# Where the two operands of a matmul lie in SBUF: a two-layer decoder trunk whose feed-forward stages get new start addresses

## The chip, the cores and the metric

The kernel runs on one core of a Trainium2 chip, in one launch. The metric is the device time of that core in microseconds (us), as the median of several runs. The engines that matter here are TensorE (PE in the profile; its weight loads have a row of their own, PEld), VectorE (DVE), ScalarE (ACT) and the DMA queue that SyncE (SP) issues.

## The reference, cut to what matters

The program is a decoder trunk of two layers on 256 tokens with a model width of 1024. Each layer is a half-step feed-forward block, a mixer and a second half-step feed-forward block. So there are four feed-forward blocks, and they hold most of the arithmetic:

```
def swiglu(x, w_gate, w_up, w_down):
    return (jax.nn.silu(x @ w_gate) * (x @ w_up)) @ w_down
...
        h = h + 0.5 * swiglu(rms_norm(h, ffn1_norm_g[layer]), ffn1_w_gate[layer],
                             ffn1_w_up[layer], ffn1_w_down[layer])
        hn = rms_norm(h, mix_norm_g[layer])
...
        h = h + jnp.concatenate([primary, mem_out], axis=-1) @ w_o[layer]
        h = h + 0.5 * swiglu(rms_norm(h, ffn2_norm_g[layer]), ffn2_w_gate[layer],
                             ffn2_w_up[layer], ffn2_w_down[layer])
```

The inner width of a block is 2816, so `w_gate` and `w_up` are 1024 x 2816 and `w_down` is 2816 x 1024, all float32. The mixers are a convolution beside attention to a memory (layer 0) and block attention beside attention to a memory (layer 1). A key and value projection stands between the layers.

## The kernel before, in words

**Split operands.** Every large product is made in float32r from a high and a low part of each operand. A weight arrives by DMA in chunks of 128 x 2048 (tile `raw`), and each half of a chunk becomes a tile `wh` (high part, written by ACT in line 214) and a tile `wl` (what is left, written by DVE in line 218), both 128 x 1024, four buffers each. The activations are held transposed, tokens along the free axis, as tiles with a high and a low part side by side: `y` with eight k-slices of 2 x 256 elements (function `y_tiles`), and `hs`, the gated inner activations, with 22 such slices.

**The matmuls of a feed-forward block.** `mm2` makes one k-step of one output tile from two matmuls. The first has a 128 x 128 block of `wh` as its stationary operand and streams the whole slice of `y` or `hs`, high and low part: 512 columns. The second has the block of `wl` and streams the high part alone: 256 columns. These are called the hi step and the lo step here. Each matmul needs its own stationary block, so hi steps and lo steps alternate and a weight load stands between any two matmuls. A block has 22 gate tiles and 22 up tiles of 8 k-steps (352 pairs), and 8 output tiles of the down product with 22 k-steps. Seven of these use `mm2` (154 pairs), and the last uses `mm3`: three matmuls of 256 columns per k-step, with stationary `wh`, `wh`, `wl` (66 matmuls). The names in the profile are `ag`, `au`, `ao` for gate, up and down of the first block, and `b`, `c`, `d` for the others. All matmuls go through a helper in line 183.

**Other matmuls.** In the mixers and the key and value projections (`A`, `B`, `C`, `Q`, `M`, `mkv`, `kv`, `mqJ`, `b0J` to `b2J`) the roles are the other way round: a block of the activations is the stationary operand, and `wh` or `wl` is streamed, 512 or 256 columns at a time. The two output projections (`oao`, `obo`) use `mm3` with weights stationary and the tile `cat` streamed, 256 columns each.

**Where the tiles lie.** `y_tiles` allocates a buffer that is 128 elements longer than needed and starts the data `at` elements in: 8 by default, 0 for `ay0`, `by0` and the memory tiles, 16 for `cy0`. The build lays the tiles out so. Addresses are in bytes within a partition, modulo 512, and in brackets modulo 128:

| operand | base | start before |
|---|---|---|
| `wh`, all four buffers | 288 | 288 (32) |
| `wl`, all four buffers | 288 | 288 (32) |
| `y0`, `oay`, `by1`, `oby`, `cat` | 288 | 320 (64) |
| `hs` of the four blocks | 192 | 192 (64) |
| `ay0`, `by0`, `my` | 288 | 288 (32) |
| `cy0` | 288 | 352 (96) |

k-slices are 2048 bytes apart and weight blocks 512 bytes, so every step of a stage has the same places modulo 512.

**Order.** The four blocks are traced in a scheduler's order. The two mixers are written out by hand (`MIX0`, `MIX1`), and there the steps named `hi16` to `hi19` of `MIX1` already convert the first weights of the fourth block.

Of the kernel before, what the change touches and what calls it, by code (L numbers as in the profile page):

```python
# [10 lines left out]
F32R = mybir.dt.float32r  # L11
# [6 lines left out]
P = 128  # L18
DM = 1024
KD = DM // P  # L20
SEQ = 256
NT = SEQ // P
DFF = 2816
KF = DFF // P
# [14 lines left out]
HC = 1024  # L39
# [70 lines left out]
NSPEC = 4 * PW  # L110

Y_AT = {"ay0": 0, "by0": 0, "cy0": 16}

@with_exitstack
def tile_kernel(ctx: ExitStack, tc: tile.TileContext, w, xT, memT, pos, vec, hg, const, wave, bias, taps, out):
    nc = tc.nc
    cp = ctx.enter_context(tc.tile_pool(name="cp", bufs=1))
    wp = ctx.enter_context(tc.tile_pool(name="wp", bufs=3))
# [32 lines left out]
    nc.vector.memset(mhalf, -0.5)  # L151


    state = {"chunk": 0, "half": 0, "raw": None, "order": "", "last": {}, "between": None, "made": []}

    def behind(i, other):
        tc.add_manual_dep(i.ins, other.ins.name,
# [11 lines left out]
    def A(i):  # L169
        return in_order("A", i)  # L170

    def V(i):
        return in_order("V", i)
# [4 lines left out]
    def tables(func):  # L178

        behind(A(nc.scalar.activation(warm, onec, func)), state["func"])  # L180

    def mmul(*a, **k):
        return in_order("P", nc.tensor.matmul(*a, **k))  # L183
# [7 lines left out]
    def load_chunk(n):  # L191
        if n == 0:
            return raw0
        raw = wp.tile([P, CH], F32, name=f"raw{n}", tag="raw", bufs=3)
        if n < 3:
            nc.sync.dma_start(raw[:, :HC], w[n][:, :HC])
            state["sync"] = nc.sync.dma_start(raw[:, HC:], w[n][:, HC:])
        else:
            state["sync"] = nc.sync.dma_start(raw, w[n])
        return raw  # L200

    def half_hi():
        n, h = state["chunk"], state["half"]
        if h == 0:
            state["raw"] = load_chunk(n)
        raw = state["raw"][:, h * HC:(h + 1) * HC]
        wh = wp.tile([P, HC], F32R, name=f"wh{n}_{h}", tag="wh", bufs=4)
        wl = wp.tile([P, HC], F32R, name=f"wl{n}_{h}", tag="wl", bufs=4)
        state["chunk"], state["half"] = (n, 1) if h == 0 else (n + 1, 0)
        q = HC // 2 if n < 2 else HC  # L210
        parts = [slice(c, c + q) for c in range(0, HC, q)]

        def hi(s):
            state["act"] = nc.scalar.activation(wh[:, s], raw[:, s], AF.Copy)  # L214
            return state["act"]

        def lo(s):
            state["dve"] = nc.vector.tensor_tensor(wl[:, s], raw[:, s], wh[:, s].bitcast(F32), op=ALU.subtract)  # L218
            return state["dve"]
        return wh, wl, parts, hi, lo  # L220
# [16 lines left out]
    def mm3(o, wt, y, k, first, last, **kw):  # L237
        h, l = wt
        i = mmul(o, h, y[:, k, 0], start=first, stop=False, **kw)
        mmul(o, h, y[:, k, 1], start=False, stop=False, **kw)  # L240
        mmul(o, l, y[:, k, 0], start=False, stop=last, **kw)
        return i

    def mm2(o, wt, y, k, first, last, turn=None):

        h, l = wt
        a = mmul(o, h, y[:, k].rearrange("p a s -> p (a s)"), start=first, stop=False)
        if turn is not None:
            state["between"] = a
            turn()  # L250
            last_turn, state["between"] = state["between"], None
        b = mmul(o[:, :SEQ], l, y[:, k, 0], start=False, stop=last)
        if turn is not None:
            behind(b, last_turn)
# [9 lines left out]
    def both_halves(name, o, tag):  # L264

        c = tp.tile([P, SEQ], F32, name=name + "c", tag="cvq")
        nc.scalar.activation(c, o[:, SEQ:], AF.Copy)
        a = tp.tile([P, SEQ], F32, name=name, tag=tag)
        nc.vector.tensor_tensor(a, o[:, :SEQ], c, op=ALU.add)
        return a  # L270

    def mm3_tok(o, wh, wl, y, t, k, c, first, last):
        s = slice(t * P, (t + 1) * P)
        mmul(o, y[:, k, 0, s], wh[:, c], start=first, stop=False)
        mmul(o, y[:, k, 0, s], wl[:, c], start=False, stop=False)
        mmul(o, y[:, k, 1, s], wh[:, c], start=False, stop=last)

    def psum(name, tag="mm", bufs=4):
        return ps.tile([P, 512], F32, name=name, tag=tag, bufs=bufs)


    def y_tiles(name, at=8):

        n = KD * 2 * SEQ
        y = yp.tile([P, n + P], F32R, name=name, tag="y")
        return y[:, at:at + n].rearrange("p (k h s) -> p k h s", k=KD, h=2)
# [11 lines left out]
    def square_sum(name, acc, src, first, adder=nc.gpsimd):  # L298
        if first:
            nc.scalar.activation(acc, src, AF.Square)  # L300
        else:
            sq = tp.tile([P, SEQ], F32, name=name, tag="sq")
            nc.scalar.activation(sq, src, AF.Square)
            adder.tensor_tensor(acc, acc, sq, op=ALU.add)
# [32 lines left out]
    def new_acc(name):  # L337
        return tp.tile([P, SEQ], F32, name=name, tag="acc")

    def ffn(name, y, acc, nexts, store=False, hook=None, after=None, hook_down=None, r=None, plan=None):  # L340


        plan = plan or {}
        rows_at = [j for (j, _, _), what in plan.items() if what == "rows"]
        hs = cp.tile([P, KF, 2, SEQ], F32R, name=name + "hs", tag="hs")
        first = acc is None
        rb = None if r is None else bcast_rows(name + "nb", r)
        halves = {}
# [22 lines left out]
        for j in range(KF):  # L371
# [4 lines left out]
            if first and j == 0:  # L376
# [21 lines left out]
                n = KD  # L398
# [9 lines left out]
            else:  # L408

                at = ("sc", 2) if first and j == 2 else ()  # L410
# [21 lines left out]
            for i in sorted(halves):  # L432
                g, h = halves.pop(i)
                if i > 1 or not rows_at:
                    g, h = both_halves(f"{name}gs{i}", g, "g"), (lambda i=i, h=h: both_halves(f"{name}h{i}", h, "h"))
                gated(i, g, h, rb)
        if after:
            tables(after)
        ys = [y_tiles(f"{name}y{i}", Y_AT.get(f"{name}y{i}", 8)) for i in range(len(nexts))]
        acc = new_acc(name + "acc")  # L440
        it = tiles_of(KD * KF // 8)
        for m in range(KD):
            po = psum(f"{name}o{m}")
            if hook_down:
                with tc.issue_after(state["act"].ins):
                    hook_down(m)

            both_sums = m < KD - 1
            for k in range(KF):
                if both_sums:  # L450
                    mm2(po, next(it), hs, k, k == 0, k == KF - 1)
                else:
                    mm3(po[:, :SEQ], next(it), hs, k, k == 0, k == KF - 1)
            if both_sums:
                d = both_halves(f"{name}d{m}", po, "g")
                nc.vector.scalar_tensor_tensor(d, d, 0.5, rb, op0=ALU.mult, op1=ALU.mult)
            else:
                d = tp.tile([P, SEQ], F32, name=f"{name}d{m}", tag="g")
                nc.vector.scalar_tensor_tensor(d, po[:, :SEQ], 0.5, rb, op0=ALU.mult, op1=ALU.mult)
            nc.vector.tensor_tensor(x[:, m], d, x[:, m], op=ALU.add)  # L460
            if store:
                nc.sync.dma_start(out[m], x[:, m])
                continue
            for yy, g in zip(ys, nexts):
                state["ends"] = scaled_split(yy, x[:, m], m, g)
            square_sum(f"{name}q{m}", acc, x[:, m], m == 0)
        return ys, acc

    def heads_norm(name, t, n):
# [32 lines left out]
    def proj(name, y, *uses):  # L502

        os_ = [psum(f"{name}{t}") for t in range(NT)]
        n = MW * len(uses)
        per = HC // n
        for k0 in range(0, KD, per):
            wh, wl = half_chunk()
            for t in range(NT):
                for i in range(per):  # L510
                    k = k0 + i
                    mm3_tok(os_[t][:, :n], wh, wl, y, t, k, slice(i * n, (i + 1) * n), k == 0, k == KD - 1)
        for t in range(NT):
            for i, use in enumerate(uses):
                use(t, os_[t][:, i * MW:(i + 1) * MW])
# [193 lines left out]
    y = y_tiles("y0")  # L709
# [123 lines left out]
    for i in range(HEAD1):  # L833
        @step(f"hi{i}")
        def _(i=i):
            halves[i] = half_hi()
            for s in halves[i][2]:
                j = A(halves[i][3](s))
            if i == HEAD0 + 1:
                behind(j, state["ends"][0])  # L840
# [291 lines left out]
    ys = y_tiles("oay")  # L1132
# [6 lines left out]
    y = ys  # L1139
# [17 lines left out]
    ys = y_tiles("oby")  # L1157
# [4 lines left out]
    for i in range(20):  # L1162
        @step(f"hi{i}")
        def _(i=i):
            halves[i] = half_hi()
            for s in halves[i][2]:
                j = A(halves[i][3](s))
            if i == 4:
                behind(j, state["ends"][0])
            if i >= 16:  # L1170
                state["made"].append(halves[i][:2])

        @step(f"lo{i}")
        def _(i=i):
            for s in halves[i][2]:
                j = V(halves[i][4](s))

            if i == 3:
                behind(j, state["ends"][1])
# [167 lines left out]
    y, acc = ys, sums  # L1347
# [162 lines left out]
```

## Time and profile before

| | us |
|---|---|
| median of 3 runs | 959.43 |
| lowest and highest | 958.76, 960.69 |
| the profiled execution, its own time | 958.8 |
| its span, first to last instruction | 956.8 |
| PE busy | 950.2 |
| PEld busy | 833.0 |
| DVE busy | 719.1 |
| ACT busy | 561.8 |

The profile is of one execution. The spans of matmuls overlap, because a matmul starts before the one before it has drained. So the length of one row is not what a matmul costs: that is the distance from its start to the start of the next, called a step here. The chain of work that ended last merges matmuls that follow each other into pieces, and a piece divided by its count is the mean step.

### The profile page before, as it was taken

The page shows a single profiled execution, that of the slowest core. Times are in us where ns is not written, and L with a number is a line of the kernel's source. Part 1 is how long each engine was busy: PE and PEld are TensorE (multiplying, and loading weights), DVE is VectorE, ACT ScalarE, POOL GpSimd, SP SyncE. Part 2 cuts the span into 40 slices and gives each one's busy share as a digit, 9 for nine tenths or more (in the row PEclk, how much of TensorE's full clock was granted, in tenths as well). Part 3 has the DMA queues.
Part 4 walks back from the last instruction along what each step waited for, and adds up shares of the span by engine and source line. Part 5 has one row for each costly group of instructions (what it writes and reads, how often), then busy time and mean ns, then how long its engine had stood idle before and what let it go on. Part 6 is the DMA issues. An engine that isn't in the chain of part 4 may idle for free.

```text
span 956.8 us, 15067 instructions
## 1 busy us (share of the span) xinstructions
PE 950.2 (99%) x5699; PEld 833.0 (87%) x5699; DVE 719.1 (75%) x1243; ACT 561.8 (59%) x1026; POOL 103.1 (11%) x101
## 2 busy tenths in 40 slices
PE   9999999999999999999999999999999999999998
PEld 6888888888789888888988888888997998888887
DVE  7888877767887877767767777767779578777663
ACT  6676666554566665555556665555548666556442
POOL 0122000112223000001123000000134120000000
PEclk9999999999999999999999999999999999999999
DMA  8755555554334655555555455555542245555560
GB/s 326 272 197 181 176 190 205 178 182 170 133 132 166 216 191 179 195 199 176 192 194 188 176 187 205 181 183 202 187 177 79 99 176 188 208 177 184 199 215 19
DMA packets 26936, 174.16 MB, mean 182 GB/s; under 512 B 3376, under 2 KB 5136, under 8 KB 6512
## 3 DMA queue, kind: packets, MB, share of 16 engines
q1 hardware_dynamic: 26576, 173.04, 51.4%
q8 instruction: 44, 0.72, 0.3%
q14 instruction: 28, 0.23, 0.1%
q10 hardware_dynamic: 288, 0.17, 0.1%
HBM read 172.15 MB, written 1.05 MB: 181 GB/s over the span
## 4 chain that ended last, share of the span: by engine, by line
PE 96%; DVE 3%; ACT 0%; POOL 0%; issue 0%; ACTq 0%
PE ag L183 6%; PE au L183 6%; PE do L183 6%; PE co L183 6%; PE bo L183 6%; PE ao L183 6%; PE bg L183 6%; PE dg L183 6%; PE cg L183 6%; PE cu L183 6%; PE bu L183 6%; PE du L183 6%; PE kv L183 3%; PE obo L183 2%; PE oao L183 2%; PE A L183 1%
## 5 line engine op out<-in xcount | busy, mean ns | idle before, releaser
L214 ACT ACTIVATE wh<-raw 128x1024 fp32r<-128x1024 f32 (+1 forms) x326 | 341.8, 1050 | 339.5 <-PE dg L183 26.8
L218 DVE TENSOR_TENSOR wl<-raw,wh 128x1024 fp32r<-128x1024 f32 (+1 forms) x326 | 396.5, 1218 | 178.2 <-ACT wh L214 176.9
L183 PE MATMUL ag<-y,wh 128*128 128x512 f32 x176 | 63.7, 396 | 0.0
L183 PE MATMUL au<-y,wh 128*128 128x512 f32 x176 | 63.2, 392 | 0.0
L183 PE MATMUL bg<-oay,wh 128*128 128x512 f32 x176 | 62.4, 391 | 0.0
L183 PE MATMUL dg<-oby,wh 128*128 128x512 f32 x176 | 62.4, 391 | 0.0
L183 PE MATMUL bu<-oay,wh 128*128 128x512 f32 x176 | 62.2, 390 | 0.0
L183 PE MATMUL du<-oby,wh 128*128 128x512 f32 x176 | 62.2, 390 | 0.0
L183 PE MATMUL cg<-by,wh 128*128 128x512 f32 x176 | 62.2, 391 | 0.0
L183 PE MATMUL cu<-by,wh 128*128 128x512 f32 x176 | 62.1, 391 | 0.0
L183 PE MATMUL bo<-bhs,wh 128*128 128x512 f32 (+1 forms) x198 | 61.1, 367 | 0.0
L183 PE MATMUL ao<-ahs,wh 128*128 128x512 f32 (+1 forms) x198 | 61.1, 367 | 0.0
L183 PE MATMUL co<-chs,wh 128*128 128x512 f32 (+1 forms) x198 | 61.1, 367 | 0.0
L183 PE MATMUL do<-dhs,wh 128*128 128x512 f32 (+1 forms) x198 | 61.1, 367 | 0.0
L183 PE MATMUL cg<-by,wl 128*128 128x256 f32 x176 | 49.8, 283 | 0.0
L183 PE MATMUL bg<-oay,wl 128*128 128x256 f32 x176 | 49.7, 282 | 0.0
L183 PE MATMUL dg<-oby,wl 128*128 128x256 f32 x176 | 49.7, 282 | 0.0
L183 PE MATMUL du<-oby,wl 128*128 128x256 f32 x176 | 49.6, 282 | 0.0
L183 PE MATMUL cu<-by,wl 128*128 128x256 f32 x176 | 49.6, 282 | 0.0
L183 PE MATMUL bu<-oay,wl 128*128 128x256 f32 x176 | 49.6, 282 | 0.0
L183 PE MATMUL ag<-y,wl 128*128 128x256 f32 x176 | 49.6, 284 | 0.0
L183 PE MATMUL au<-y,wl 128*128 128x256 f32 x176 | 49.4, 283 | 0.0
(948 smaller groups left out, 2309.6 us busy)
## 6 DMA issues: line engine op xcount, KB each, us to landing
raw<-in_w SPq DMA_DIRECT2D x158, 1024.0 KB, 4.8
raw<-in_w SPq DMA_DIRECT2D x5, 512.0 KB, 8.2
mT<-in_memT SPq DMA_DIRECT2D x1, 1024.0 KB, 8.3
out<-x SPq DMA_DIRECT2D x8, 128.0 KB, 1.8
raw<-in_w SPq DMA_DIRECT2D x2, 256.0 KB, 4.0
x<-in_xT SPq DMA_DIRECT2D x1, 512.0 KB, 6.6
spec<-in_bias SPq DMA_DIRECT2D x1, 384.0 KB, 9.8
tapw<-in_taps SPq DMA_DIRECT2D x1, 288.0 KB, 9.1
```

Source lines behind the costliest of these rows:

```text
L183: return in_order("P", nc.tensor.matmul(*a, **k))
L214: state["act"] = nc.scalar.activation(wh[:, s], raw[:, s], AF.Copy)
L218: state["dve"] = nc.vector.tensor_tensor(wl[:, s], raw[:, s], wh[:, s].bitcast(F32), op=ALU.subtract)
```

## The change

Three places get new start addresses. `y_tiles` starts its data 16 elements in by default (64 bytes, before: 32). The gated activations `hs` start 40 elements in (160 bytes, before: 0), in a tile that is 512 bytes longer. The tiles `wl` are 512 bytes longer, and in the feed-forward blocks their data starts 16 elements in. A variable in `state` switches that on at the start of a block and off at its end; the projections that `proj` makes in the middle of a block switch it off for themselves, and the last four conversions of `MIX1`, which belong to the fourth block, switch it on.

```
-    def y_tiles(name, at=8):
+    def y_tiles(name, at=16):
...
 Y_AT = {"ay0": 0, "by0": 0, "cy0": 16}
+LOW_AT, GATED_AT = 16, 40
...
         wh = wp.tile([P, HC], F32R, name=f"wh{n}_{h}", tag="wh", bufs=4)
-        wl = wp.tile([P, HC], F32R, name=f"wl{n}_{h}", tag="wl", bufs=4)
+        wl = wp.tile([P, HC + P], F32R, name=f"wl{n}_{h}", tag="wl", bufs=4)[:, state["low_at"]:state["low_at"] + HC]
...
+        state["low_at"] = LOW_AT
         plan = plan or {}
         rows_at = [j for (j, _, _), what in plan.items() if what == "rows"]
-        hs = cp.tile([P, KF, 2, SEQ], F32R, name=name + "hs", tag="hs")
+        n = KF * 2 * SEQ
+        hs = cp.tile([P, n + P], F32R, name=name + "hs", tag="hs")
+        hs = hs[:, GATED_AT:GATED_AT + n].rearrange("p (k h s) -> p k h s", k=KF, h=2)
...
-        ys = [y_tiles(f"{name}y{i}", Y_AT.get(f"{name}y{i}", 8)) for i in range(len(nexts))]
+        ys = [y_tiles(f"{name}y{i}", Y_AT.get(f"{name}y{i}", 16)) for i in range(len(nexts))]
...
+        state["low_at"] = 0
         return ys, acc
...
+        low_at, state["low_at"] = state["low_at"], 0
         for k0 in range(0, KD, per):
             wh, wl = half_chunk()
...
+        state["low_at"] = low_at
...
+            if i >= 16:
+                state["low_at"] = LOW_AT
             halves[i] = half_hi()
```

The build then has these starts modulo 512 (modulo 128 in brackets); `wh`, `ay0`, `by0`, `my` and `cy0` keep theirs:

| operand | base after | start after |
|---|---|---|
| `wl` in the feed-forward blocks | 288 | 352 (96) |
| `wl` elsewhere | 288 | 288 (32) |
| `y0`, `oay`, `by1`, `oby`, `cat` | 288 | 352 (96) |
| `hs` of the four blocks | 192 | 352 (96) |

On every engine the same instructions stand in the same order as before.

More of the change, by code (lines that the diff above doesn't have):

```diff
@@ L151, in tile_kernel @@
     nc.vector.memset(mhalf, -0.5)
-    state = {"chunk": 0, "half": 0, "raw": None, "order": "", "last": {}, "between": None, "made": []}
+    state = {"chunk": 0, "half": 0, "raw": None, "order": "", "last": {}, "between": None, "made": [], "low_at": 0}
     def behind(i, other):
```

## The prediction

> **What bounds the kernel now.** I read the page first: the busy shares, the granted clock and the chain of work that ended last.
>
> ```profile
> span 956.8 us, 15067 instructions
> PE 950.2 (99%) x5699; PEld 833.0 (87%) x5699; DVE 719.1 (75%) x1243; ACT 561.8 (59%) x1026; POOL 103.1 (11%) x101
> ...
> PEclk9999999999999999999999999999999999999999
> ...
> PE 96%; DVE 3%; ACT 0%; POOL 0%; issue 0%; ACTq 0%
> ```
>
> TensorE is 96% of the chain, at full clock from end to end. There is hardly a wait to remove, so the time moves only if matmuls follow each other faster or slower. Since "a busy PE is not PE at its peak", the next view is the chain in order of time, where a piece divided by its count is the mean step from one matmul's start to the next. First a stretch of the second block's gate and up products, where a piece of 16 is eight pairs of a hi and a lo step:
>
> ```profile
> 321.11 2.77 PE bu L183 x16
> 323.88 2.77 PE bg L183 x16
> 326.65 2.77 PE bu L183 x16
> ```
>
> 2.77 / 8 = 346.3 ns per pair, piece after piece without a gap. Then the timeline of PE and its weight loads in the fourth block, to see what runs beside a stream:
>
> ```profile
> 886.12 0.39 PE L183 MATMUL dg<-oby,wh 128*128 128x512 f32 x1
> 886.12 0.19 PEld L183 LDWEIGHTS dg<-oby,wl 128*128 128x128 f32 x1
> 886.35 0.28 PE L183 MATMUL dg<-oby,wl 128*128 128x256 f32 x1
> 886.35 0.19 PEld L183 LDWEIGHTS dg<-oby,wh 128*128 128x128 f32 x1
> 886.47 0.39 PE L183 MATMUL dg<-oby,wh 128*128 128x512 f32 x1
> ```
>
> When the hi step starts streaming 512 columns of `oby`, the load of the next block, from `wl`, starts in the same 10 ns. When the lo step starts streaming 256 columns, the load of the next `wh` starts. So TensorE reads two SBUF places at once, and the pair of places is fixed: streamed activation against `wl` under a hi step, against `wh` under a lo step. I call the start of the streamed operand minus the start of the block loaded beside it, modulo 128 bytes, the offset. From the table of starts it is 32 in every feed-forward step before (64 - 32). After, a hi step has offset 0 (96 - 96), a lo step 64 (96 - 32).
>
> The question is whether a step depends on the offset. This kernel holds other offsets already, where activations are loaded and weights streamed:
>
> ```profile
> 205.53 9.57 PE A L183 x42
> 219.66 8.18 PE B L183 x36
> 227.84 2.87 PE Q L183 x24
> ...
> 501.41 10.69 PE kv L183 x47
> ...
> 703.57 5.45 PE b0J L183 x48
> ```
>
> `Q` and `b0J` do the same products of 256 columns from the same kinds of tiles. `Q` loads from `ay0` (start 32 modulo 128, streamed `wh` and `wl` at 32): offset 0, 2.87 / 24 = 119.6 ns. `b0J` loads from `cy0` (start 96): offset -64, which is 64 modulo 128, and 5.45 / 48 = 113.5 ns. `A`, `B` and `kv` stream 512 columns at offset 0: 227.9, 227.2 and 227.4 ns. For 256 columns at the feed-forward offset of 32, the output projection of the first mixer and the last tile of the fourth block's down product (62 matmuls within a window) have rows of their own, and the two whole down products beside them give the hi step:
>
> ```profile
> 272.59 11.21 PE oao L183 x96
> ...
> 418.17 61.15 PE bo L183 x374
> ...
> 891.83 61.16 PE do L183 x374
> ```
>
> ```profile
> 945.35 7.28 PE do L183 x62
> ```
>
> 11.21 / 96 = 116.8 ns and 7.28 / 62 = 117.4 ns. A down product is 154 pairs and 66 steps of 256: (61.15 - 66 x 0.1174) / 154 = 346.7 ns per pair, so its hi step takes 346.7 - 117.4 = 229.3 ns. For gate and up the same subtraction with 116.8 gives 229.5 ns.
>
> So, by rows: 256 columns take 119.6 at offset 0, about 117 at 32, 113.5 at 64; 512 columns take 227.3 at 0, about 229.4 at 32, and no row shows 64.
>
> **The change, part by part.** It adds, removes and moves no instruction; it changes addresses. The sum is made against the profiled execution, 958.8 us (span 956.8 and 2.0 around it). The median of the three runs is 959.4, 0.6 higher, and the forecast carries that 0.6.
>
> *Gate and up.* 352 pairs in each of four blocks are 1408. The new pair is 227.3 (offset 0, 512 columns) plus 113.5 (offset 64, 256 columns) = 340.8 ns. 1408 x (346.3 - 340.8) = 7.7 us. The first 32 of these pairs, in block `a`, go four hi steps together and then four lo steps, so most offsets there are the other way round, and I take their 0.2 us off: 7.5 us.
>
> *Down products.* 154 pairs in four blocks are 616: 616 x (346.7 - 340.8) = 3.6 us. Here `hs` moves from 192 to 352 modulo 512. The rows of `hs` and `y` before differ by 128 bytes modulo 256, and 117.4 stands against 116.8, 229.3 against 229.5: a shift by 128 has cost at most 0.6 ns. That is my ground for counting offsets modulo 128, and for taking 64 to be as good as -64.
>
> *The last down tile.* Of three steps of 256 columns, two load `wh` (offset 64) and one loads `wl` (offset 0). 4 x 44 x (117.4 - 113.5) = 0.7 us gained, 4 x 22 x (119.6 - 117.4) = 0.2 us lost: 0.5 us.
>
> *Output projections.* `cat` goes to 96, both weight parts stay at 32 there, so all steps have offset 64: 2 x 192 x (116.8 - 113.5) = 1.3 us. Part of them stands among hand-ordered work that waits on other engines, so I count 0.9.
>
> *Unaffected.* `kv`, `A` to `C`, `Q`, `M` and `b0J` keep their starts; `proj` switches the shift off.
>
> *Who must keep up.* ACT writes `wh` and DVE writes `wl`, the latter to new addresses.
>
> ```profile
> L214 ACT ACTIVATE wh<-raw 128x1024 fp32r<-128x1024 f32 (+1 forms) x326 | 341.8, 1050 | 339.5 <-PE dg L183 26.8
> L218 DVE TENSOR_TENSOR wl<-raw,wh 128x1024 fp32r<-128x1024 f32 (+1 forms) x326 | 396.5, 1218 | 178.2 <-ACT wh L214 176.9
> ```
>
> ```profile
> 0.00:25.00 25.00, 23.56 (x116) 17.31 (x117) 18.46 (x34) 16.65 (x31) 0.89 (x5) 1.00 0.91 324
> ...
> 294.00:414.00 120.00, 120.00 (x700) 106.52 (x699) 93.75 (x157) 73.27 (x136) 7.91 (x8) 1.00 0.55 193
> ```
>
> ACT sits idle before line 214 because it waits for PE to free a buffer, so the conversions are ahead of PE. In the second block's gate and up stage (columns: PE, PEld, DVE, ACT, POOL, clock, DMA share, GB/s) DVE is busy 93.75 of 120 us. A DVE slowed by up to 120 / 93.75 = 1.28 would still be hidden; without that cover each further per cent would cost some 5 us over the four blocks. The weights come at 193 GB/s and would have to come at 193 x 346.3 / 340.8 = 196; the first 25 us show 324. Both are costed at nothing.
>
> Sum: 7.5 + 3.6 + 0.5 + 0.9 = 12.5 us. 958.8 - 12.5 = 946.3, plus 0.6: **946.9 us**.
>
> How wide is this? The gain on the lo steps (2024 of them, 3.3 to 3.9 ns) is over half of the sum and rests on 64 being like -64. The hi steps (2.0 to 2.2 ns, 4.3 us) rest on an activation streamed at offset 0 being like a weight streamed at offset 0. With 1 ns more or less on both kinds of step, 2024 x 2 ns = 4.0 us, the forecast's own range is 943 to 951.
>
> **The rivals.**
>
> *Direction counts.* The known good place has the streamed operand 64 behind the loaded one, the new one 64 ahead. If the pattern repeats only after 512 bytes, 64 is an unseen value between 32 (117) and the rest of the circle, and the lo step may stay at 117. Then only the hi steps gain: 2024 x 2.1 = 4.3 us, less the 0.2 of the last tile: 955.3. For it: no row shows +64. Against it: the step hardly moved when `hs` and `y` differed by 128.
>
> *Nothing changes.* `Q` and `b0J` also differ in loop order (tokens inside k against k inside a half) and in what the other engines do at the time. If that made the 6 ns, the offset does nothing and the time stays 959.4. Against it: `b0J` and the last down tiles, both of 256 columns and both going through k in order, differ as well, 113.5 against 117.4, and the down rows of blocks `b` and `d` agree within 0.01 us although the engines beside them do different work. The Trainium skill, page "TensorE: Matmul & The Clock Gate", section "Step-by-step: what each phase is for", speaks for this rival and against the change: it says that weight loads and the streamed operand have a read port each, so that a load takes no read bandwidth from a running matmul. By that rule the time would be 959.4; `Q` at 119.6 against `b0J` at 113.5 does not agree.
>
> *Slower: level is the bad place.* Among the rows of 256 columns offset 0 is the worst, 119.6, and the change puts every hi step there. `A`, `B` and `kv` look fine at 0, but they stream weights and load activations. If a level load costs a streamed activation what it costs in `Q`, 119.6 - 116.8 = 2.8 ns, and 64 does not help the lo steps, the four blocks lose 2024 x 2.8 = 5.7 us: 965. With a gain of 3.3 ns on the lo steps it turns slower only once the hi step is above 229.4 + 3.3 = 232.7 ns.
>
> *More than forecast.* The ten bf16 warm-up matmuls and their like show what 512 columns take when little is read beside them:
>
> ```profile
> 8.82 1.74 PE pw L183 x8
> ```
>
> 1.74 / 8 = 217.5 ns. If a better place took the hi step down to that, 2024 x (227.3 - 217.5) = 20 us more would go: 927. A part of it, to about 938, is possible, since no row shows a 512-column stream of an activation at 0. The same page of the Trainium skill, section "Back-to-back issue gap", gives columns / 2.4 + 2.5 ns, which is an estimate of 215.8 and 109.2 ns for the two steps; the trace's pair of 346.3 lies 21 ns above that.
>
> **How the numbers follow.** Chances: forecast 0.64 (946.9), direction counts 0.14 (955.3), nothing 0.07 (959.4), slower 0.09 (965), more than forecast 0.06 (938). A difference of 0.2%, 1.9 us, is about what a measurement of this kernel can tell from no change. Faster by more: 0.64 + 0.14 + 0.06 = 0.84. Within it: 0.07. Slower: 0.09. The range takes in the forecast's own and the direction rival, and reaches a little below the former: 941 to 956. It leaves out the rivals "nothing" and "slower" and most of "more": 0.07 + 0.09 + 0.04 = 0.20.
>
> **What would show it.** Right: in the profile after, pieces of 16 in gate and up read 2.72 to 2.73 us where they read 2.77, the whole down products 60.1 to 60.2 where they read 61.15, the first `oao` piece 10.9 where it reads 11.21, and `Q`, `b0J`, `B` and `kv` as before. The direction rival reads 2.75 and leaves `oao` at 11.2. Nothing changed reads 2.77. The slower rival reads 2.79 or more. Wrong in another way would be: pieces shorter, but DVE or a DMA ending waits of PE in the blocks, which would mean that the cover above was thinner than I took it for.

## The result, and the profile after

The changed kernel takes 946.21 us in the median of 4 runs (945.83 to 947.53), against 959.1 us before (4 runs). The ratio is 0.9867, with a 95% interval of 0.9849 to 0.9884. The forecast was 946.9 us. The profiled execution took 945.9 us, with a span of 943.9.

The page of the profile after: TensorE is still the whole chain, at full clock, and the writers of the weights cost what they did.

```profile
span 943.9 us, 15067 instructions
...
PE 937.4 (99%) x5699; PEld 823.5 (87%) x5699; DVE 718.5 (76%) x1243; ACT 562.3 (60%) x1026; POOL 104.0 (11%) x101
...
PEclk9999999999999999999999999999999999999999
...
PE 96%; DVE 3%; ACT 0%; POOL 0%; issue 0%; ACTq 0%
...
L219 DVE TENSOR_TENSOR wl<-raw,wh 128x1024 fp32r<-128x1024 f32 (+1 forms) x326 | 396.7, 1218 | 167.1 <-ACT wh L215 165.9
```

The chain after, in order of time: a stretch of the second block's gate and up products. A piece of 16 is eight pairs.

```profile
319.91 2.72 PE bg L184 x16
322.63 2.72 PE bu L184 x16
325.35 2.72 PE bg L184 x16
```

2.72 / 8 = 340 ns per pair, where 346.3 stood. The longest pieces of the same view, over the whole span:

```profile
201.77 9.53 PE A L184 x42
215.87 8.18 PE B L184 x36
224.05 2.87 PE Q L184 x24
...
268.80 11.31 PE oao L184 x96
280.55 10.25 PE oao L184 x87
...
412.39 60.17 PE bo L184 x374
...
494.60 10.68 PE kv L184 x47
...
509.63 2.80 PE cu L184 x16
512.43 2.80 PE cg L184 x16
515.23 2.80 PE cu L184 x16
...
693.74 5.45 PE b0J L184 x48
...
879.92 60.18 PE do L184 x374
```

The down products went from 61.15 to 60.17 us. `A`, `B`, `Q`, `kv` and `b0J` kept their lengths within 0.04 us. Three things were not forecast. The first output projection's piece got longer, 11.21 to 11.31 us. At the start of the third block eight pairs take 2.80 us, 350 ns per pair: more than before the change, with the same addresses as the 340. And the last tile of the fourth block's down product, 62 matmuls of 256 columns within a window, takes 7.30 us where it took 7.28:

```profile
932.43 7.30 PE do L184 x62
```

By the first starts of the matmuls of each stage, from the first gate to the first down matmul, the four gate and up stages went from 138.7, 123.8, 122.8 and 127.0 us to 136.1, 121.6, 120.8 and 124.9: 8.9 us together. The down products gave 3.9 us. The rest of the span gained 0.1. That makes the 12.9 us between the spans of 956.8 and 943.9.

### The profile page after: what moved, and what is told of

Read it like the earlier page. It is cut to its first block, busy times and chain, and to the rows that moved or that the text cites. A ratio compares the mean times of both kernels' runs of the same rounds, so it can differ in the third digit from the quotient of the medians.

```text
span 943.9 us, 15067 instructions
## 1 busy us (share of the span) xinstructions
PE 937.4 (99%) x5699; PEld 823.5 (87%) x5699; DVE 718.5 (76%) x1243; ACT 562.3 (60%) x1026; POOL 104.0 (11%) x101
## 4 chain that ended last, share of the span: by engine, by line
PE 96%; DVE 3%; ACT 0%; POOL 0%; issue 0%; ACTq 0%
PE au L184 6%; PE do L184 6%; PE co L184 6%; PE bo L184 6%; PE ao L184 6%; PE dg L184 6%; PE ag L184 6%; PE bg L184 6%; PE cg L184 6%; PE cu L184 6%; PE du L184 6%; PE bu L184 6%; PE kv L184 3%; PE obo L184 2%; PE oao L184 2%; PE M L184 1%
## 5 line engine op out<-in xcount | busy, mean ns | idle before, releaser
L219 DVE TENSOR_TENSOR wl<-raw,wh 128x1024 fp32r<-128x1024 f32 (+1 forms) x326 | 396.7, 1218 | 167.1 <-ACT wh L215 165.9
```

## The experiments

### Longer buffers, old places

```
-LOW_AT, GATED_AT = 16, 40
+LOW_AT, GATED_AT = 0, 0
...
-    def y_tiles(name, at=16):
+    def y_tiles(name, at=8):
...
-Y_AT.get(f"{name}y{i}", 16)
+Y_AT.get(f"{name}y{i}", 8)
```

> The buffers stay as long as in the changed kernel, so every tile behind them lies where it lies there, but all data starts where it started before: offset 32 in every feed-forward step. Theory (the offset between the streamed start and the start of the block loaded beside it sets the step): as before the change, 959 us, pieces of 16 in gate and up at 2.77 us. Rival (the new pitch of the low parts or the moved tiles make the gain): as after, 946 us, 2.72 us.

958.88 us; ratio to before 1.0001 (0.9991 to 1.001). The chain has the old pieces:

```profile
320.81 2.77 PE bu L184 x16
323.58 2.77 PE bg L184 x16
```

The new pitch and the moved tiles do nothing. The start addresses make the gain.

### The parts of the move, one by one

Three kernels change the table of places, each an edit of the same constants.

In the first the low parts are not moved:

```
-LOW_AT, GATED_AT = 16, 40
+LOW_AT, GATED_AT = 0, 40
```

> As changed, but the low parts start where they did before: hi steps and lo steps both at offset 64. Theory: the lo step stays at 113.5 ns; the hi step moves away from the 227 ns of offset 0, and the few hi steps that have another hi step behind them in the changed kernel (offset 64, about 230 ns) say where to: pieces of 16 at 2.75 us, about 952 us. Rival (only the lo step matters, the low parts need not have moved): 946 us, 2.72 us. Rival of the prediction (offset 0 is the bad place for a hi step): faster than the changed kernel, below 945 us.

970.09 us; ratio 1.012 (1.0105 to 1.0135).

```profile
322.14 2.82 PE bg L184 x16
324.96 2.83 PE bu L184 x16
```

In the second everything is level, with `y_tiles` at 0:

```
-LOW_AT, GATED_AT = 16, 40
+LOW_AT, GATED_AT = 0, 24
```

> The streamed operands start level with high and low parts alike, everything at 32 modulo 128: hi steps and lo steps at offset 0, the output projections too. Theory: the hi step is as in the changed kernel, 227 ns, the lo step as Q, 119.6 ns, so 346.6 ns per pair and 2.77 us per piece of 16, with the output projections 1 us slower: 959 to 961 us. Rival (the gain comes from being level with the low parts, whatever the high parts do): 946 to 948 us, 2.72 us.

966.11 us; ratio 1.0077 (1.006 to 1.0094).

In the third the low parts alone are moved, with `y_tiles` at 8:

```
-LOW_AT, GATED_AT = 16, 40
+LOW_AT, GATED_AT = 16, 0
```

> Only the low parts move: hi steps at offset -32 (96 modulo 128), lo steps at 32 as before. Theory: the lo step stays at 117 ns, the hi step is at an offset that no row shows, between 227 and 230 ns, so 2.75 to 2.78 us per piece and 954 to 960 us. Rival (moving the low parts away from the high parts makes the gain by itself): 946 us, 2.72 us.

966.48 us; ratio 1.0078 (1.0063 to 1.0093).

All three are slower than before, and not one landed where the theory put it. The steps in the feed-forward blocks say why. With the low parts not moved, the lo step has the offset 64 of the changed kernel, but its mean is 119.2 ns instead of 114.0. With everything level, the hi step has the offset 0 of the changed kernel, but its mean is 233.4 ns instead of 227.0 (means from start to start, stalls left out). So the offset of a step does not set its length. The steps that the prediction took from `Q`, `b0J`, `B` and `kv` and added up were the wrong kind of quantity. What these runs leave standing is that the pair as a whole has a length, which the grids below look at.

### Moving everything, or the streamed operand alone

First all three places of the feed-forward blocks 32 bytes later, with `y_tiles` at 24 and `wh` 8 elements into a longer buffer (`cat` stays as in the changed kernel):

```
-LOW_AT, GATED_AT = 16, 40
+LOW_AT, GATED_AT = 24, 48
```

> In the feed-forward blocks streamed operands, high parts and low parts all start 32 bytes later than in the changed kernel (0, 64 and 0 modulo 128), so every offset between them is as there. Theory (only the differences of the places count, and how the run began): 340 ns per pair, 2.72 us per piece of 16, about 946 us. Rival (places by themselves count, for example a start at 32 or 96 modulo 128): another pair, 2.75 us or more.

946.34 us; ratio 0.9863 (0.9848 to 0.9878), pieces of 2.72 us. The time is that of the changed kernel, so over this shift of 32 bytes only the distances between the three places count.

Then the streamed operands alone 128 bytes later, with `y_tiles` at 48:

```
-LOW_AT, GATED_AT = 16, 40
+LOW_AT, GATED_AT = 16, 72
```

> The streamed operands start 128 bytes later than in the changed kernel, high and low parts stay: offsets of 128 and 192 where they were 0 and 64. Theory (the pattern repeats after 128 bytes, so 192 is like -64 and like 64): 340 ns per pair, 2.72 us, about 946 us. Rival of the prediction (direction counts, the pattern is longer than 128 bytes): lo steps off 113 ns, pieces of 2.75 us or more, 952 us and up.

969.5 us; ratio 1.0105 (1.0089 to 1.0122).

```profile
320.47 2.83 PE bg L184 x16
323.29 2.83 PE bu L184 x16
```

A shift of 128 bytes is not nothing: 353 ns per pair here. In the first and fourth block about half of the gate and up pairs ran at 347. Counting offsets modulo 128, on which the forecast for the lo step rested, was wrong.

### Interruptions

```
+        def pause(kind, j):
+            def turn():
+                pb = psum(f"{name}pause{kind}{j}", "aux", 2)
+                for i in range(2):
+                    if kind == "T":
+                        transp(pb[:, i * P:(i + 1) * P], ident, ident)
+                    else:
+                        m = mmul(pb[:, i:i + 1], ident, onec, start=True, stop=True)
...
+            plan = {**plan, **{(j, "g", 3): pause("ST"[i % 2], j) for i, j in enumerate((8, 10, 12, 14, 16, 18))}}
```

> As changed, with twelve short interruptions of TensorE, six in the second and six in the fourth block, between a hi and a lo step, four gate-and-up tiles apart: by turns two matmuls of one column and two transposes. Their products are not used. Each adds some 0.25 us, 3 us in all. In the changed kernel stretches with the same addresses run at 340 or at 350 ns per pair, and switch where such matmuls come between. Theory (the addresses allow two rhythms, and the way a run begins picks one): some of the twelve stretches of 32 pairs run at 2.80 us per piece and others at 2.72, switching at the interruptions alone; 949 to 951 us. Rival (the 350 ns come from what other engines do in those places): all stretches at 2.72 us, 949 us.

952.76 us; ratio 0.9929 (0.9914 to 0.9943). The chain in the second block; `bpauseS` are the matmuls of one column, `bpauseT` the transposes:

```profile
336.92 1.25 PE bg L184 x7
338.18 0.34 PE bpauseS L184 x4
338.52 1.63 PE bg L184 x9
340.15 2.80 PE bu L184 x16
342.95 2.80 PE bg L184 x16
345.75 2.80 PE bu L184 x16
348.55 1.28 PE bg L184 x7
349.83 0.22 PE bpauseT L187 x2
350.05 1.50 PE bg L184 x9
351.54 2.72 PE bu L184 x16
354.26 2.72 PE bg L184 x16
```

The same places run at 350 or at 340 ns per pair, and the rhythm holds until TensorE is interrupted. All six interruptions by matmuls of one column led to 31 pairs at 350. All six by transposes led to 340 again, four of them after three pairs near 345. The six slow stretches cost 6 x 31 x 10 ns = 1.9 us. The other 4.7 us are 0.39 us per interruption, where 0.25 was expected. So the slow pieces at the start of the third block can be a rhythm that the work before them left behind, without any other engine.

The kind of the interruption is not the whole of it. In the changed kernel, at the start of the third block, two transposes between two pairs (`cnbp`) stand ahead of the 350, and two transposes inside a pair (`sk2p`) end it:

```profile
509.41 0.22 PE cnbp L187 x2
509.63 2.80 PE cu L184 x16
...
519.66 0.22 PE sk2p L187 x2
519.88 1.14 PE cg L184 x7
521.02 2.72 PE cu L184 x16
```

And after matmuls of one column between two pairs (`bnrp`, `dnrp`), the second block went on with 11 pairs at 350 and the fourth with 9 at 340.

### Two grids of places

Two kernels leave the reference's computation out and run only pairs of a hi and a lo step, or steps of 256 columns, on converted weights that stay where they are. Each ran once, at a granted clock of 1.0. The last instruction of VectorE or ScalarE starts at 15.3 us of 700.4 in the first and at 15.0 of 1129.3 in the second, so what these two write plays no part in the cells below.

```
+    for kind in "TS":
+        for sn, s in at.items():
+            for ln, l in at.items():
+                ys = slices(s)
...
+                        mmul(o, wh[:, c], ys[:, k].rearrange("p a s -> p (a s)"), start=k == 0, stop=False)
+                        mmul(o[:, :SEQ], wl[:, c], ys[:, k, 0], start=False, stop=k == KD - 1)
```

> The reference's computation is left out: TensorE alone repeats the hi and lo steps of a feed-forward block, 48 pairs for each of 16 pairs of places (streamed operand 0, 32, 64 or 96 bytes behind the high parts, low parts 0, 32, 64 or 96 behind the high parts), once begun with two transposes and once with two matmuls of one column, and then 24 triples of 256 columns for each. First theory, of the prediction (a step depends on its own offset): pair times are a sum of a part from the hi offset and a part from the lo offset, so the four cells with hi offset 0 differ from each other only as the lo offsets do. Second theory (the rhythm of the whole pair locks on one of a few lengths): no such sum; cells take one of a few values, 340 ns among them, and nothing lies below 340. Places as changed (64, 64): 340 ns; as before (32, 0): 346.7; both 64 and 0: 349 to 357.

The pair of places (64, 64) of the changed kernel, begun with transposes (`vTcc`) and with matmuls of one column (`vScc`), and the place (64, 0) (`vTca`), in the chain in order of time; a piece of 95 is 47 pairs and one lo step:

```profile
149.67 16.72 PE vTca L149 x95
...
183.81 16.57 PE vTcc L149 x95
```

```profile
457.49 16.22 PE vScc L149 x95
```

Mean pair times from start to start, the interrupted pair and the two behind it left out, after transposes / after matmuls of one column, in ns. Rows: streamed operand behind the high parts, in bytes; columns: low parts behind the high parts.

| | 0 | 32 | 64 | 96 |
|---|---|---|---|---|
| 0 | not counted / 346.7 | 346.7 / 346.6 | 346.7 / 346.7 | 346.7 / 351.7 |
| 32 | 346.8 / 346.8 | 344.5 / 344.6 | 353.3 / 349.0 | 346.7 / 346.7 |
| 64 | 353.2 / 353.4 | 348.9 / 348.8 | 350.0 / 340.0 | 347.0 / 346.9 |
| 96 | 350.0 / 350.0 | 353.3 / 353.3 | 346.7 / 346.7 | 349.4 / 349.3 |

The first cell begins with pairs of 640 ns, 427 and 213 for the two steps, and is left out. By the first theory a pair is a part from the hi offset (row minus column) and a part from the lo offset (row). Then one row down and one column to the right, which keeps the hi offset, would add the same everywhere. But from (32, 0) to (64, 32) the time rises by 2 ns, and from (32, 64) to (64, 96), begun with transposes, it falls by 6. The kernel before sat at (32, 0): 346.8 in the grid, 346.3 to 346.7 in its trace. (64, 64) is the one place with 340, and it has 350 too. Here, unlike in the run with interruptions, it was the transposes that led to 350.

> The reference's computation is left out, as in the grid before: 24 pairs of a hi and a lo step for each of 64 pairs of places, streamed operand and low parts each 0, 64, ... 448 bytes behind the high parts, begun once with two transposes and once with two matmuls of one column. Reading of the prediction (the pattern repeats after 128 bytes): the table has only four kinds of cells, and all with odd multiples of 64 on both sides run at 340 or 350 ns as (64, 64) does. Rival (the pattern is longer, so the changed kernel's 64 ahead was not the known 64 behind): moving the streamed operand by 128 leaves the fast rhythm, near 353 ns at (192, 64), and only some cells repeat (64, 64). A cell that runs at 340 ns after both kinds of beginning would be a better place for the kernel; nothing should lie below 340.

The corner up to 192 bytes, in the same form:

| | 0 | 64 | 128 | 192 |
|---|---|---|---|---|
| 0 | not counted / 346.6 | 346.6 / 346.7 | 346.6 / 346.6 | 349.9 / 351.1 |
| 64 | 353.2 / 348.9 | 340.0 / 340.0 | 353.4 / 346.6 | 346.6 / 346.7 |
| 128 | 351.0 / 351.2 | 346.7 / 346.8 | 352.0 / 351.8 | 346.6 / 347.2 |
| 192 | 352.9 / 352.9 | 353.4 / 350.0 | 353.3 / 352.1 | 349.9 / 340.0 |

Three rows of the chain, begun with transposes: (64, 64), (320, 320) and (192, 192), 47 steps each.

```profile
91.61 7.95 PE vTbb L149 x47
...
246.62 8.17 PE vTdd L149 x47
...
401.78 7.97 PE vTff L149 x47
```

Adding 256 bytes to one or both places left the time within 1 ns in 88 of 93 comparisons; adding 128 did so in 34 of 93. In nearly all cells the pattern repeats after 256 bytes. 340 ns exists where streamed operand and low parts are level and stand 64 or 192 bytes behind the high parts, modulo 256, and no cell lies below it. The second place reached it after one kind of beginning only. (64, 64) reached it after both, where the first grid had 350 after transposes: the kind of beginning alone does not decide.

### The other side of the circle, in the kernel

`y_tiles` starts at 48, and `cat` stays as in the changed kernel.

```
-LOW_AT, GATED_AT = 16, 40
+LOW_AT, GATED_AT = 48, 72
```

> Streamed operands and low parts both start 128 bytes later than in the changed kernel, so they stay level with each other, and stand 192 bytes behind the high parts (64 ahead of them, going round 256 bytes). Theory of the second grid (the pattern repeats after 256 bytes; fast where the streamed operand is level with the low parts and 64 or 192 behind the high parts): 340 ns per pair in most of the blocks and 350 where a block begins badly, 946 to 951 us. Rival (only 64 ahead works, moving by 128 is bad by itself, as moving the streamed operand alone was): 353 ns and 969 us.

964.18 us; ratio 1.0053 (1.0037 to 1.0069). Gate and up of the second block, then its down product and that of the fourth:

```profile
324.80 2.83 PE bg L184 x16
...
420.91 60.49 PE bo L184 x374
...
896.45 61.69 PE do L184 x374
```

One down product found the fast rhythm, with 125 of its 154 pairs at 340 ns, and a part of the first block did. Most stages ran at 348 to 357 ns. Both readings missed. The fast rhythm exists there, but the kernel's stages rarely fall into it, so in this kernel 64 behind and 64 ahead are not worth the same.

### The output projections

```
-            late["cat"] = y_tiles("cat0")
+            late["cat"] = y_tiles("cat0", 48)
...
-    cat = y_tiles("cat1")
+    cat = y_tiles("cat1", 48)
```

> As changed, but the tile that the two output projections stream starts 192 instead of 64 bytes behind both weight parts. Where that place was run, the steps of the first output projection had a mean of 115.7 ns and those of the second 114.8, against 117.8 and 117.3 in the changed kernel. Theory (a run of 256-column steps has its own places, apart from those of the pairs): 192 x 2.1 + 192 x 2.5 ns = 0.9 us less in the trace, 945.3 us, and the first piece of 96 at 11.1 us instead of 11.31. Rival (those steps got shorter there because of how the runs began): no change, 946.2 us.

945.77 us; ratio 0.9859 (0.9842 to 0.9877), which overlaps the interval of the changed kernel: not told apart. In the trace the first piece stays, and the second is shorter than the changed kernel's 10.25 us:

```profile
269.21 11.31 PE oao L184 x96
280.96 9.88 PE oao L184 x87
```

Same places, same tile, two rhythms again, so the place alone does not set these steps. In this run `b0J`, whose own places did not move, went from 5.45 to 5.65 us, 117.7 ns per step:

```profile
693.90 5.65 PE b0J L184 x48
```

### Gate and up alone

```
+        state["low_at"] = 0
         it = tiles_of(KD * KF // 8)
```

with `GATED_AT` 0 and `cat` at 8, so that down products and output projections have their old places.

> Only the gate and up products have the changed places; the down products and the output projections have their places of before the change. By the trace of the changed kernel, whose gate and up stages are 8.9 us shorter than before, whose down products are 3.9 us shorter and whose output projections are some 0.1 us longer: 950 us, pieces of 16 at 2.72 us, down products at 61.15 us. Rival (one stage's rhythm carries into the next, so the parts don't add): down products off 61.15 us by more than 0.3 us, or a time off 950 by more than 2 us.

949.94 us; ratio 0.9907 (0.989 to 0.9923).

```profile
270.48 11.21 PE oao L184 x96
413.86 61.15 PE bo L184 x374
```

The parts add: 8.8 us here (958.73 before, in the same runs), and the down products of the first three blocks keep their 61.15 us within 0.01.

## Why the prediction was right, point by point

**The bound.** Right. TensorE's rhythm is the time, and 12.8 of the 12.9 us are in the steps of the feed-forward blocks.

**Gate and up, 7.5 us.** 8.9 measured. Of it 0.5 lies in the first 32 pairs, which the forecast left out. There three early hi steps took 427, 426 and 272 ns before and 236, 229 and 231 after; in the run with gate and up alone, at the new places, they took 427, 426 and 298, so this part is not the places' doing. In the rest, 8.4 us, the pair went to 340.0 ns and not to 340.8, and some 60 pairs run at 350.

**Down products, 3.6 + 0.5 us.** 3.9 measured, but not in these parts. The pairs gave 4.0 us (616 pairs, on average from 346.78 to 340.23 ns). The last tiles, forecast to gain 0.5, lost 0.1: their steps went from 117.3 to 117.8 ns.

**Output projections, 0.9 us.** Wrong in sign: 11.21 became 11.31 us. The step carried 113.5 ns from `b0J` to a run of the same width and, modulo 128, the same offset. In the first grid the runs of 256 columns had means of 117 to 120 ns at all sixteen places. And the 113.5 is no property of `b0J`'s places: with them unchanged it became 117.7 when `cat` was moved, and in the changed kernel `b2J`, at an unchanged place, has mostly steps of 117 and 118 ns where it had 113 and 114 before. So these steps have rhythms too.

**The sum.** 12.5 us forecast, 12.9 between the spans. It came out close because two terms that were too small (gate and up, the down pairs) made up for two of the wrong sign (the last tiles, the output projections). That the number came out so close was luck.

**The offset sets each step.** This step of the prediction failed, although its number came out. The pair is what has a length, and it depends on three places at once: 64 behind the high parts is worth 340 ns with the low parts level and 353 with the low parts not moved. The rows of `Q`, `b0J`, `B` and `kv` pointed to the right cause and were no measure of how much.

**Modulo 128, so 64 is like -64.** Failed as well. The ground given was that `hs` and `y`, 128 bytes apart, had almost equal steps; they stood 32 and 160 behind the high parts, modulo 256, with the low parts at 0. It held for those two and not in general: from (0, 0) to (128, 0) the grid goes from 346.6 to 351.2. The rival "direction counts" was right that the pattern is longer than 128 bytes, and wrong that the lo step would therefore stay at 117 ns. That the new place was good was luck as far as this argument goes.

**Slower, because level is bad.** Level with both parts is slower, 966.1 us. Level with the low parts alone, both 64 behind the high parts, is the fast place. The rival named a real cost at the wrong place.

**Nothing changes.** Refuted. In the feed-forward blocks the low parts are only loaded and never streamed, and moving their starts alone makes 23.9 us (970.09 against 946.21). The Trainium skill, page "TensorE: Matmul & The Clock Gate", section "Step-by-step: what each phase is for", gives weight loads a read port of their own, which takes nothing from the running matmul. By that, the place of a loaded block would make no difference to the stream beside it; the 23.9 us do not agree. Whether the ports have a part in it, no run shows.

**More than forecast.** Did not come: no cell of either grid lies below 340 ns.

**Cover.** Right: the producer's line costs 1218 ns as before, and ACT still waits for PE.

What stays open is the mechanism. The runs show which lengths occur at which places. They do not show what is shared inside the memory or the array, nor why the same kind of beginning led to 350 ns in one kernel and to 340 in another.

## What to carry to other kernels

Where TensorE runs without gaps, take the step from start to start and try start addresses of the streamed operand and of the loaded blocks against each other, in steps of 32 bytes over 256: here the range was 340 to 353 ns per pair, 4%. Try the places together, in the kernel itself: no place could be judged alone, and moving the streamed operand or the low parts by themselves was slower than moving nothing. A neighbour stage with another order of matmuls shows that places matter, not which one is good.

## What the runs showed of the hardware that was not expected

Many of the pair times fall on a few lengths: 340.0, 346.7, 350.0 and 353.3 ns among them. Patterns of one to three pairs repeat without change until something comes between, for example hi steps of 237, 231 and 234 ns in turn at (64, 0). Two lengths can belong to the same addresses. Then what came before decides, and the rhythm holds: 31 pairs at 350 ns after each of six interruptions, and at least 28 at 340 after each of the six others. Which beginning leads to which rhythm stays open.
